# Hybrid attention encoder layer: a planner that tells an engine's occupation from the lag of its result

## The chip, the cores and the metric

The kernel runs on one core of a Trainium2 chip. The metric is the device time of one execution in microseconds (us). Before the change three runs took 2861.65, 2861.87 and 2867.31 us; their median is 2861.87 us. One more execution was profiled, and every row shown below is of that one.

## The reference, cut to what matters

The layer takes two sequences, `x_sample` of 2048 tokens and `x_prompt` of 512, each with 1024 features, and one set of weights. Everything is float32.

```python
h = rms_norm(x, norm_gain)
proj = h @ w_in                          # 1024 -> 9216, split in 16 parts
q_a, k_a = rms_norm per head             # 8 heads of 64
o_a = neighborhood_attention(q_a, k_a, v_a, rel_bias_a)   # 8 rows x 16 columns of a grid of width 64
for (window, dil) in ((128, 1), (512, 4), (2048, 16)):    # three dilated groups
    q, k = rope(rms_norm(...))
    o, lse = sliding window attention over tokens of stride dil
o_b = sum over groups of softmax(lse) * o
br_a = (o_a * silu(g_a)) @ w_branch_a    # 512 -> 1024
br_b = (o_b * silu(g_b)) @ w_branch_b
merged = sigmoid(m_a) * br_a + sigmoid(m_b) * br_b
y = x + merged @ w_out                   # 1024 -> 1024
```

## The kernel before, in words

**Stages.** `run` (L2065) calls four sweeps. `dil_sweeps` takes tiles of 128 tokens, 20 for each of the three dilated groups; for each it makes three products of 512 columns (q, k, v) and the attention of the tokens that are complete by then. `na_sweeps` takes 40 tiles (two halves of four heads, 20 tiles each) with a q-and-k product of 512 columns and a v product of 256, and the neighbourhood attention. `gate_sweeps` makes gates and branch products in blocks of 256 tokens, `out_sweep` the last product. The float32 products are made as three products of 16-bit parts (a high and a low part of each side), so that one bank of 512 columns over 1024 features is 24 matmuls.

**What a q or k tile passes through** (`dil_qk`, L1390): TensorE fills a PSUM tile `proj` (four exist). ScalarE copies it to `qk` and squares it to `sq` (these two give the `proj` tile back), VectorE sums the squares (`q_ssq`), GpSimd turns it by the rope tables (two halves `sq<-qk,gcs`, then `qk<-qk,gcs`, then `qk<-qk,sq`), computes the last step of the inverse root on small tiles (`q_c`, `q_t`, `q_y`) and scales (`qk<-qk,q_y`); ScalarE writes the high half `qs`, VectorE or GpSimd the low half, and a transposing DMA on SyncE's queue carries `qs` to `dq` or `kT`. Three `qk` tiles exist.

**What a unit of attention passes through** (`head` L764, `softmax` L801, `pump` L854): the scores go to a PSUM tile `s` (two exist); VectorE adds the mask and takes the maximum (a custom instruction, `e<-s,cmask` or `e<-s,bm`), ScalarE or VectorE makes `neg`, ScalarE takes exp in place, ScalarE or VectorE writes the high half `p`, VectorE or GpSimd the low half (two `e` tiles exist; one is held from the maximum to here), a transposing DMA carries `p` to `pT` (six exist), and the products with v go to `o`.

**What sets the order of the work.** The order of instructions on each engine is the order in which the Python program emits them; nothing reorders it afterwards, and each engine takes its own instructions strictly in that order. The program finds the order with a model of time, `Clock`. The sweeps emit TensorE's matmuls one after the other and advance `clk.t` by each one's cost (`pe`, L130). Every other step is an event on a heap: it is emitted when TensorE's model time has passed the time at which the step's inputs are ready (`at` L119, `then` L123, `catch_up` L148). `run` (L134) books a step on its engine: the engine is taken for the step's cost, and the result is ready a lag after that; the next step of the chain becomes an event at that time (`done`). Buffers (`Slots`) are given back in model time too, and `first` (L144) chooses between two engines by which would be done first. `dma` (L138) books an issue on the queue, then a cost on one shared resource `D`, then a lag. So the constants of the model change no instruction's work; they change where a step stands among others on its engine, and now and then which of two engines takes a step.

**Names that the steps below use.** `mm` L351 (cost of a matmul), `act` L359, `vec` L364, `pool` L376, `copy` L368 and `either` L380 (the two that choose an engine), `turn` L398 (transposing DMA), the margins `M_T = 0.5` (before a transpose of `p`) and `M_PV = 1.5` (after it, before the product with v), and the pace of units of attention, `DIL_STEP` and `NA_STEP`. None of the margins and paces is touched. All helper lines of the profile (L352, L360, L365, L377, L400) lie in these functions, so that groups are told apart by their tiles.

Of the kernel before, what the change touches and what calls it, by code (L numbers as in the profile page):

```python
# [13 lines left out]
F32 = mybir.dt.float32  # L14
# [11 lines left out]
D = 1024  # L26
# [59 lines left out]
NA_P = 0.7  # L86
DIL_STEP = 1.3
DIL_1 = 0.8
LAG_A = 0.6
LAG_V = 0.35  # L90
LAG_P = 0.2
LAG_D = 1.2
A_DMA = 0.1
NA_ACT = 0
# [9 lines left out]
PORT = 0.18  # L104
BIAS_STEP = 4.0
LAG = {"A": LAG_A, "V": LAG_V, "P": LAG_P, "D": LAG_D}


class Clock:
# [25 lines left out]
        self.free[e] = max(self.now, self.free[e]) + cost  # L135
        self.done = self.free[e] + LAG[e]

    def dma(self, e, issue, cost):  # L138

        self.free[e] = max(self.now, self.free[e]) + issue  # L140
        self.free["D"] = max(self.free[e] + 0.7, self.free["D"]) + cost
        self.done = self.free["D"] + LAG["D"]

    def first(self, **costs):  # L144

# [29 lines left out]
class Slots:  # L175
# [37 lines left out]
    def new(self, pool, shape, dtype, names):  # L213

        i = self.granted.popleft()
        pool = self.pools.get(i, pool)
        if i in self.views:
            ts = [self.views[i]]
        else:
            ts = [pool.tile(shape, dtype, name=self.names.get(i, f"{n}{i}"), bufs=1) for n in names]  # L220
        self.where[self.key(ts[0])] = i
        return ts
# [38 lines left out]
def size(ap):  # L261
    return math.prod(ap.shape[1:])


class Enc:
# [84 lines left out]

    def mm(self, out, a, b, start, stop, share=1, **kw):  # L351
        self.nc.tensor.matmul(out, a, b, start=start, stop=stop, **kw)  # L352
        self.clk.pe((size(b) * (4 if b.dtype == F32 else 1) / 2400 + 0.003) / share)

    def tp(self, out, x, m=128):
        self.nc.tensor.transpose(out, x, self.ident[:m, :m])
# [2 lines left out]
    def act(self, out, x, func=AF.Copy, **kw):  # L359
        self.nc.scalar.activation(out, x, func, **kw)  # L360
        by_row = not isinstance(kw.get("scale", 1.0), float) or "bias" in kw
        self.clk.run("A", 0.155 + size(out) / 1200 + 0.135 * by_row + 0.28 * ("accum_out" in kw))

    def vec(self, ins, /, out, *a, n=None, more=0.0, **kw):  # L364
        getattr(self.nc.vector, ins)(out, *a, **kw)  # L365
        self.clk.run("V", 0.15 + (n or size(out)) / 960 + 0.08 * ("accum_out" in kw) + more)

    def copy(self, out, x):  # L368

        n = size(out)  # L370
        if self.clk.first(A=0.155 + n / 1200, V=0.15 + n / 1920 + PORT) == "A":
            self.act(out, x)
        else:
            self.vec("tensor_copy", out, x, n=n / 2, more=PORT)

    def pool(self, ins, /, out, *a, n=None, **kw):  # L376
        getattr(self.nc.gpsimd, ins)(out, *a, **kw)  # L377
        self.clk.run("P", 0.23 + (n or size(out)) / 480)

    def either(self, ins, /, out, *a, n=None, **kw):  # L380

        n = n or size(out)
        if self.clk.first(V=0.15 + n / 960 + PORT, P=0.23 + n / 480) == "V":
            self.vec(ins, out, *a, n=n, more=PORT, **kw)
        else:
            self.pool(ins, out, *a, n=n, **kw)
# [11 lines left out]
    def turn(self, out, in_):  # L398

        self.nc.sync.dma_start(out=out, in_=in_, transpose=True)  # L400
        n = math.prod(out.shape)
        self.clk.dma("S", max(1.23, n / 107e3), n / 82e3)

    def new(self, name, shape, dtype=F32, pool=None, names=None):
        ts = self.S[name].new(pool or self.P.get(name) or self.ps, shape, dtype, names or (name,))
# [317 lines left out]
    def split_v(self, R, ps, nh, pool, name, then):  # L723

        clk = self.clk
        ps3 = ps.rearrange("p (h d) -> p h d", d=64)

        def high():
            R["v"], = self.S[name].new(pool(), [128, nh, 2, 64], FP16, (name,))
            self.act(R["v"][:, :, 0], ps3, scale=VP)  # L730
            clk.then(low)

        def low():
            self.vec("scalar_tensor_tensor", R["v"][:, :, 1], ps3, VP, R["v"][:, :, 0], op0=ALU.mult,
                     op1=ALU.subtract)
            self.S["proj"].give(ps)
            clk.then(then)

        self.S[name].take(high)
# [61 lines left out]
    def softmax(self, u):  # L801
# [33 lines left out]
        def low():  # L835
            p = u["p"]
            self.either("tensor_tensor", p[:m, N:2 * N], u["e"][:m, :N], p[:m, :N], op=ALU.subtract)
            S["e"].give(u["e"])
            clk.at(clk.done + M_T, S["pT"].take, turn)
# [166 lines left out]
    def na_qk(self, R, seq, i, ps):  # L1006
# [102 lines left out]
        moved.when(lambda: S["qs"].give(R["qs"]))  # L1109
        there.when(groups)  # L1110
        S["qk"].take(copy)

    def na_group(self, seq, g):
# [276 lines left out]
    def dil_qk(self, R, i, ps):  # L1390
# [51 lines left out]
        def low():  # L1442
            self.either("tensor_tensor", *B["parts"][1], op=ALU.subtract)
            S["qk"].give(B["x"])
            clk.then(R["place", i].when, turn)

        def turn():
# [3 lines left out]
            R["ch"]["done"][R["i"]].signal()  # L1451

        S["qk"].take(copy)

    def dil_v(self, R, ps):
# [212 lines left out]
    def gate_o(self, H, br, blk):  # L1668
# [27 lines left out]
        def low(tt, o, qs):  # L1696
            self.either("tensor_tensor", qs[:, 512:1024], o, qs[:, 0:512], op=ALU.subtract)
            S["x"].give(o)
            clk.then(turn, tt, qs)
# [476 lines left out]
```

## Time and profile before

| what | value |
|---|---|
| median of three runs | 2861.87 us |
| the profiled execution's own time | 2864.63 us |
| its span, first to last instruction | 2862.8 us |
| TensorE busy | 2675.4 us (93%) |
| GpSimd, VectorE, ScalarE busy | 1474.7, 1576.5, 1334.6 us |
| chain of waits, share by engine | PE 65%, DVE 9%, POOL 8%, DMA 7%, ACT 6% |
| mean granted TensorE clock | 0.971 |

In the rows PE is TensorE's matmuls, PEld its weight loads, DVE VectorE, ACT ScalarE, POOL GpSimd and SPq SyncE's queue, which issues all the DMAs. Times are from the start of the span. The sweeps of the dilated groups fill the span up to some 1245 us, the neighbourhood attention up to some 1806 us, the gates up to 2636 us, the last product the rest. A row of the view of waits says who sat idle until whose result came, for how long in total, how often, and the longest.

### The profile page before, as it was taken

How to read it: one execution, taken by the hardware profiler on the slowest of the kernel's cores; microseconds unless marked ns; L12 is line 12 of the kernel's file. 1: busy time of each engine (PE TensorE's matmuls, PEld its weight loads, DVE VectorE, ACT ScalarE, POOL GpSimd, SP SyncE). 2: the span in 40 equal slices, each digit the busy share in tenths (PEclk: the TensorE clock that was granted, in tenths of full speed). 3: DMA queues.
4: the chain of work that ended last, by engine and by line, in shares of the span. 5: the costliest groups of instructions: out<-in, count | busy, mean ns of one | idle time of the engine just before them, and what ended most of it. 6: DMA issues, size and time to landing. Idle time of an engine off the chain costs nothing.

```text
span 2862.8 us, 55914 instructions
## 1 busy us (share of the span) xinstructions
PE 2675.4 (93%) x20841; PEld 1788.6 (62%) x20841; DVE 1576.5 (55%) x3670; ACT 1334.6 (47%) x3561; POOL 1474.7 (52%) x1991
## 2 busy tenths in 40 slices
PE   5998989989999999999898886899999999999999
PEld 2444444444444444455455554889999999999887
DVE  7777666775655764557676687332145444454111
ACT  5666666665666665656666667221123121122010
POOL 4987768677778888756676664000012121131110
PEclk9999999999999999999999996899999999999999
DMA  7999886766675755588998897332144344353443
GB/s 208 223 214 195 176 196 110 158 127 119 114 121 114 156 114 115 98 224 182 192 226 190 180 206 169 85 71 75 45 129 159 109 128 133 110 172 118 148 139 110
DMA packets 808017, 419.21 MB, mean 146 GB/s; under 512 B 689728, under 2 KB 734400, under 8 KB 801344
## 3 DMA queue, kind: packets, MB, share of 16 engines
q1 hardware_dynamic: 807744, 415.63, 62.9%
q8 instruction: 163, 2.67, 0.4%
q14 instruction: 110, 0.90, 0.1%
HBM read 171.72 MB, written 79.13 MB: 88 GB/s over the span
## 4 chain that ended last, share of the span: by engine, by line
PE 65%; DVE 9%; POOL 8%; DMA 7%; ACT 6%; issue 4%; SPq 1%; DVEq 0%; POOLq 0%; ACTq 0%
PE proj L352 54%; PE s L352 10%; POOL qk L377 4%; DMA pT<-p 4%; PE o L352 2%; DVE p L365 2%; ACT e L360 2%; DVE e L365 2%; POOL sq L377 2%; DMA qn<-qs 1%; POOL q_t L377 1%; ACT sq L360 1%; DVE wm L365 1%; DVE q_ssq L365 1%; ACT qk L360 1%
## 5 line engine op out<-in xcount | busy, mean ns | idle before, releaser
L352 PEld LDWEIGHTS <-hb 128*128 128x128 f16 x6240 | 591.6, 99 | 684.6 <-issue 124.8
L352 PE MATMUL proj<-wt,hb 128*128 128x512 f16 (+2 forms) x3360 | 688.0, 357 | 26.1 <-ACT sq L360 18.0
L352 PE MATMUL proj<-wu,hb 128*128 128x512 f16 x2880 | 668.4, 385 | 45.1 <-ACT sq L360 30.5
L360 ACT ACTIVATE sg<-proj,wi 128x256 f32<-128x256 f32 x240 | 113.1, 473 | 639.3 <-PE proj L352 629.7
L360 ACT ACTIVATE e<-e,neg,sc 128x256 f32<-128x256 f32 (+4 forms) x688 | 393.4, 574 | 8.4 <-DVE neg L365 4.5
L352 PE MATMUL proj<-hb,wt 128*128 128x256 f16 x2760 | 313.7, 274 | 5.0 <-DMA hb<-htd 2.1
L352 PEld LDWEIGHTS <-pT 128*128 128x128 f16 (+1 forms) x4560 | 227.7, 102 | 139.1 <-DMA pT<-p 64.1
L352 PEld LDWEIGHTS <-wt 128*128 128x128 f16 x2760 | 269.3, 98 | 39.4 <-issue 4.0
L377 POOL TENSOR_TENSOR qk<-qk,sq 128x512 f32<-128x512 f32 (+1 forms) x141 | 183.9, 1304 | 196.2 <-DVE qk L365 100.7
L365 DVE TENSOR_TENSOR p<-e,p 128x512 f16<-128x512 f32 (+2 forms) x278 | 248.1, 893 | 63.4 <-ACT p L360 59.6
L377 POOL TENSOR_TENSOR sq<-qk,gcs 128x256 f32<-128x256 f32 x240 | 191.4, 818 | 135.6 <-DVE q_ssq L365 128.9
L365 DVE TENSOR_TENSOR qk<-s,sg 128x256 f32<-128x256 f32 x160 | 67.7, 424 | 348.1 <-PE s L352 345.6
L352 PE MATMUL s<-hb,wt 128*128 128x256 f32 x1880 | 246.9, 285 | 0.0
L352 PE MATMUL proj<-hb,kT 128*128 128x256 f16 x1920 | 228.2, 276 | 5.2 <-ACT sg L360 2.7
L352 PEld LDWEIGHTS s<-hb,wt 128*128 128x128 f32 x1880 | 231.2, 189 | 0.9
L377 POOL TENSOR_TENSOR hb<-sg,hb 128x256 fp32r<-128x256 f32 x65 | 54.0, 831 | 341.3 <-ACT hb L360 341.3
L365 DVE CUSTOM_DVE_ANT_0 e<-s,cmask 128x256 f32<-128x256 f32 (+2 forms) x528 | 154.3, 344 | 107.1 <-PE s L352 90.2
L352 PEld LDWEIGHTS <-kT 128*128 128x128 f16 x1920 | 184.4, 99 | 30.5 <-DVE kT L365 3.5
L365 DVE CAST p<-e 128x512 f16<-128x512 f32 (+2 forms) x182 | 120.1, 660 | 131.4 <-ACT e L360 109.5
L377 POOL TENSOR_TENSOR qk<-qk,q_y 128x512 f32<-128x512 f32 x160 | 179.2, 1124 | 5.2
L377 POOL TENSOR_TENSOR qk<-qk,gcs 128x512 f32<-128x512 f32 x120 | 167.0, 1391 | 9.4
L352 PE MATMUL proj<-wv,hb 128*128 128x512 f16 x660 | 156.6, 383 | 8.3 <-ACT sq L360 6.9
(181 smaller groups left out, 3774.9 us busy)
## 6 DMA issues: line engine op xcount, KB each, us to landing
hb<-htd SPq DMA_DIRECT2D x40, 1024.0 KB
wr<-in_w_in SPq DMA_DIRECT2D x132, 256.0 KB
obd<-osb SPq DMA_DIRECT2D x50, 264.0 KB
hd<-xs SPq DMA_DIRECT2D x20, 512.0 KB
htd<-hb SPq DMA_DIRECT2D x10, 1024.0 KB
mad<-qk SPq DMA_DIRECT2D x40, 256.0 KB
e<-obd SPq DMA_DIRECT2D x40, 256.0 KB
sq<-mad SPq DMA_DIRECT2D x40, 256.0 KB
```

Of the source, the lines that this page charges most:

```text
L352: self.nc.tensor.matmul(out, a, b, start=start, stop=stop, **kw)
L360: self.nc.scalar.activation(out, x, func, **kw)
L365: getattr(self.nc.vector, ins)(out, *a, **kw)
L377: getattr(self.nc.gpsimd, ins)(out, *a, **kw)
```

## The change

The lags of the three engines' results fall (ScalarE 0.6 to 0.13 us, VectorE 0.35 to 0.115, GpSimd 0.2 to 0.125), and so do the fixed parts of their costs (0.155 to 0.06, 0.15 to 0.07, 0.23 to 0.19). A transposing DMA takes the shared resource for less time (elements / 82e3 to / 105e3) and has a lag of its own of 0.2 us in place of 1.2; other DMAs keep theirs. Every matmul costs the model 4% more.

```diff
-LAG_A = 0.6
-LAG_V = 0.35
-LAG_P = 0.2
+
+LAG_A = 0.13
+LAG_V = 0.115
+LAG_P = 0.125
 LAG_D = 1.2
...
-    def dma(self, e, issue, cost):
+    def dma(self, e, issue, cost, lag=LAG_D):
 
         self.free[e] = max(self.now, self.free[e]) + issue
         self.free["D"] = max(self.free[e] + 0.7, self.free["D"]) + cost
-        self.done = self.free["D"] + LAG["D"]
+        self.done = self.free["D"] + lag
...
-        self.clk.pe((size(b) * (4 if b.dtype == F32 else 1) / 2400 + 0.003) / share)
+        self.clk.pe((size(b) * (4 if b.dtype == F32 else 1) / 2400 + 0.003) * 1.04 / share)
...
-        self.clk.run("A", 0.155 + size(out) / 1200 + 0.135 * by_row + 0.28 * ("accum_out" in kw))
+        self.clk.run("A", 0.06 + size(out) / 1200 + 0.135 * by_row + 0.28 * ("accum_out" in kw))
...
-        self.clk.run("V", 0.15 + (n or size(out)) / 960 + 0.08 * ("accum_out" in kw) + more)
+        self.clk.run("V", 0.07 + (n or size(out)) / 960 + 0.08 * ("accum_out" in kw) + more)
...
-        if self.clk.first(A=0.155 + n / 1200, V=0.15 + n / 1920 + PORT) == "A":
+        if self.clk.first(A=0.06 + n / 1200, V=0.07 + n / 1920 + PORT) == "A":
...
-        self.clk.run("P", 0.23 + (n or size(out)) / 480)
+        self.clk.run("P", 0.19 + (n or size(out)) / 480)
...
-        if self.clk.first(V=0.15 + n / 960 + PORT, P=0.23 + n / 480) == "V":
+        if self.clk.first(V=0.07 + n / 960 + PORT, P=0.19 + n / 480) == "V":
...
-        self.clk.dma("S", max(1.23, n / 107e3), n / 82e3)
+        self.clk.dma("S", max(1.23, n / 107e3), n / 105e3, 0.2)
```

## Rows read from the trace of the kernel before

**Rows 1.** The page's first part: busy time, share, instructions of each engine.

```profile
PE 2675.4 (93%) x20841; PEld 1788.6 (62%) x20841; DVE 1576.5 (55%) x3670; ACT 1334.6 (47%) x3561; POOL 1474.7 (52%) x1991
```

**Rows 2.** Busy time by stretch: start:end, length, engines, granted clock, DMA share, GB/s.

```profile
0.00:100.00 100.00, 69.34 (x334) 30.56 (x335) 69.56 (x157) 57.88 (x130) 58.40 (x75) 0.95 0.76 211
100.00:600.00 500.00, 450.23 (x3305) 220.96 (x3305) 358.40 (x823) 328.68 (x875) 393.48 (x526) 0.97 0.84 178
600.00:1245.00 645.00, 624.04 (x4673) 309.67 (x4667) 380.47 (x1045) 393.09 (x1189) 515.57 (x735) 0.99 0.63 120
1245.00:1650.00 405.00, 368.58 (x3066) 210.67 (x3066) 274.69 (x665) 250.19 (x677) 265.39 (x409) 0.97 0.92 201
1650.00:1806.00 156.00, 111.15 (x1110) 72.88 (x1109) 115.66 (x278) 107.65 (x275) 81.71 (x91) 0.73 0.89 184
1806.00:2862.80 1056.80, 1052.05 (x8366) 943.85 (x8363) 377.70 (x705) 197.12 (x418) 160.16 (x160) 1.00 0.38 115
```

**Rows 3.** TensorE's waits in 100:600, 600:1245, 1245:1650 and 1650:1806, in this order.

```profile
PE proj L352 <- ACT sq L360: 37.6, 16, 5.8
...
PE proj L352 <- ACT sq L360: 11.0, 8, 3.4
...
PE o L352 <- DMA pT<-p: 19.8, 22, 3.6
...
PE o L352 <- DMA pT<-p: 22.0, 20, 2.7
PE s L352 <- DVE mx L365: 12.5, 11, 2.1
```

**Rows 4.** ScalarE's waits in 100:1245.

```profile
ACT neg L360 <- DVE osb L365: 183.1, 139, 6.7
ACT qs L360 <- POOL qk L377: 80.1, 44, 5.9
ACT qk L360 <- PE proj L352: 72.9, 31, 5.6
```

**Rows 5.** Timeline about 172 us: start, length, instruction, [idle before it and who ended that].

```profile
165.69 4.70 PE L352 MATMUL proj<-wu,hb 128*128 128x512 f16 x21
...
171.08 2.06 DVE L365 SCALAR_TENSOR_TENSOR xs<-x,x_y,xs 128x1024 f16<-128x1024 f32 x1
...
172.04 1.23 POOL L377 TENSOR_SCALAR q_c<-q_ssq,wi 128x8 f32<-128x8 f32 x1
172.09 0.63 ACT L360 ACTIVATE qs<-qk 128x512 f16<-128x512 f32 x1 [4.02 <-POOL qk L377]
172.62 0.58 ACT L360 ACTIVATE qk<-proj 128x512 f32<-128x512 f32 x1
...
173.74 2.53 PE L352 MATMUL proj<-wu,hb 128*128 128x512 f16 x11 [3.00 <-ACT sq L360]
```

**Rows 6.** Groups by line and shape: count | busy us, mean ns | idle before.

```profile
L360 ACT ACTIVATE qk<-proj 128x512 f32<-128x512 f32 x160 | 93.2, 583 | 89.5 <-PE proj L352 84.3 <-POOL qs L377 5.0
...
L377 POOL TENSOR_TENSOR qk<-qk,gcs 128x512 f32<-128x512 f32 x120 | 167.0, 1391 | 9.4
...
L377 POOL TENSOR_SCALAR q_c<-q_ssq,wi 128x8 f32<-128x8 f32 x160 | 68.6, 429 | 30.4 <-DVE q_ssq L365 30.3
...
L365 DVE TENSOR_TENSOR p<-e,p 128x512 f16<-128x512 f32 x207 | 190.7, 921 | 40.0 <-ACT p L360 36.9
```

**Rows 7.** Timeline about 443 us: a transposing DMA and the matmuls that waited for it.

```profile
441.13 1.20 SPq L400 DMA_TRANSPOSE pT<-p  x1
...
443.83 0.56 PE L352 MATMUL o<-dv,pT 128*64 128x64 f16 x12 [2.36 <-DMA pT<-p]
```

**Rows 8.** Busy time of the instructions that touch the tiles `proj`, 1740 to 1760 us.

```profile
1740.00:1760.00 20.00, 0.00 (x0) 0.00 (x0) 0.00 (x0) 0.00 (x0) 0.50 0.75 146
```

**Rows 9.** Timeline about 1723 us: first and last step of a unit on its `e` tile.

```profile
1721.81 0.69 DVE L365 CUSTOM_DVE_ANT_0 e<-s,bm 128x512 f32<-128x512 f32 x1
...
1724.88 0.69 DVE L365 TENSOR_TENSOR p<-e,p 128x512 f16<-128x512 f32 x1
```

## The prediction, made before the changed kernel was built or timed

> **What bounds the kernel now.** I read the busy times first, then the stretches, then who waited for whom in each, then single waits in the timeline. TensorE is busy for 2675.4 of 2862.8 us [rows 1], so all that a better order of the same work can win is its idle time, 187.4 us, and some of the time at the lower granted clock. The stretches say where that lies [rows 2]. From 1806 us on, 1052.1 of 1056.8 us are busy at a granted clock of 1.00: no order helps there. The first 100 us lose 30.7 us, in the chain that loads and scales the first weights. What is left are three parts. The dilated groups lose 49.8 us in 100:600 and 21.0 us in 600:1245. The neighbourhood attention loses 36.4 us in 1245:1650, where the DMA engines are busy for 0.92 of the time. Its tail, 1650:1806, loses 44.9 us of 156.0, and the mean clock granted there is 0.73: much of it runs at 1.2 GHz in place of 2.4.
>
> The waits name the causes [rows 3]. In the dilated groups TensorE waits for ScalarE's square of an earlier q or k tile, which gives a `proj` tile back: 16 + 8 waits, 48.6 us, 2.0 us each. In the neighbourhood attention it waits for transposed `pT` (22 + 20 waits, 41.8 us, 1.0 us each), and in the tail also for the maximum that gives an `s` tile back (12.5 us). Why is the square late? ScalarE takes its instructions in order and stands idle for 183.1 us before `neg`, until VectorE's maximum, and for 80.1 us before `qs`, until GpSimd's scaling [rows 4]. One case shows it [rows 5]: the matmuls of a bank end at 170.39, yet the copy and square that empty it stand behind a `qs` whose data GpSimd has ready only at 172.09, after 4.02 us of idling; TensorE loses 3.00 us. So the order on ScalarE matters, and it comes from the model.
>
> **The change, part by part.** No instruction's work changes; each part moves steps in the order.
>
> *How near the new constants are.* For 512 columns ScalarE's result now comes 0.487 + 0.13 = 0.62 us after its start, before 0.582 + 0.6 = 1.18; the row has 583 ns [rows 6]. GpSimd's product: 1.257 + 0.125 = 1.38, before 1.50; row 1391 ns. VectorE's low half: 0.783 + 0.115 = 0.90, before 1.21; row 921 ns. Only GpSimd's smallest steps are off: 0.33 against 429 ns. A half-size transpose: 1.23 + 0.7 + 0.62 + 0.2 = 2.75 us from issue to landing, before 3.93; the trace has 443.83 - 441.13 = 2.70 [rows 7]. Step by step the new model is the better one. It knows no contention, though, and no late neighbour.
>
> *Chains.* Summing a unit of two heads of 256 keys from score to product with v (0.2 from TensorE, two maxima, `neg`, two exps, high, low, `M_T`, transpose, `M_PV`) gives 13.7 us by the old constants and 9.9 by the new. The product with v therefore moves forward by up to 3.8 us among TensorE's matmuls. A q or k tile from bank to `qs` low: 12.4 us old, 10.0 new; `qs` and the rest move forward by 2.4 us on ScalarE, past evictions of later banks.
>
> *The dilated groups.* Where a step becomes ready earlier in the model, its buffer is given back earlier and the next tile is planned more tightly; ScalarE's evictions then stand behind fewer planned bursts. Bound of the gain: 183.1 of the 263.2 us that ScalarE idles [rows 4] is for VectorE, whose results the new constants place right (0.90 against 0.921); if that share of the 48.6 us goes, 34 us. Bound of the loss: `qs` moves forward by 2.4 us while GpSimd's data come no earlier; if half as many evictions again are caught as now (12 more at 2.0 us), 24 us. Between the two I take **-6 us**, close to the middle, since nothing in the rows lies nearer to one end.
>
> *Products with v.* They come up to 3.8 us sooner, and TensorE may get to them ahead of the transpose. In 600:1245 none waits for `pT`; in the attention 42 wait, 1.0 us each. A shift that is the same for all is paid once (3.8 us), since TensorE, once late, is late for everything after. Bounds: 0, and 27 more waits of 1.0 us. I take **+4 us**, the single payment.
>
> *The attention's tail.* A unit of 512 keys holds one of two `e` tiles from maximum to low half: by the old constants 1.11 + 0.89 + 1.60 + 1.18 + 1.21 = 6.0 us, by the new 0.80 + 0.33 + 1.03 + 0.62 + 0.90 = 3.7. The trace has 1721.81 to 1725.57, 3.8 us [rows 9]. So the old model could start a pair of units every 6.0 us at most, although `NA_STEP` asks for one every 4.6, and the units it could not place among the projections were left for the end: from 1740 to 1760 no instruction touches a `proj` tile [rows 8], TensorE has attention alone. With 3.7 us the pace of 4.6 decides, and a quarter of the backlog moves back to where TensorE has projections to do. A quarter of the tail's idle 44.9 us is 11 us, and the half clock gives back some more: **-14 us**. Bounds: the whole 44.9 us; and +10, if the DMA engines, 0.92 and 0.89 busy, can't take the units earlier and they wait there instead.
>
> *Parts without a price.* The choice between engines: `either` prefers VectorE by 0.474 us in place of 0.434, `copy` prefers ScalarE by 0.03 in place of 0.015; a few steps of some 0.9 us go to VectorE, which is busy for 274.7 of 405 us in the fullest attention stretch: hidden, and if that cover is gone, 1 us each. The 4% on matmuls makes the model's TensorE slower against the other engines and undoes a little of the shift (0.2 us in a bank of 24). The lower cost on `D` lets transposes follow each other sooner in the model; SyncE's queue and its issue costs are as before. In 1245:1650 I expect nothing either way, with 20 us on both sides, as the DMA share is 0.92. The clock: each stall avoided spares some of the time at the lower level, **-2 us** (granted 0.97 in 100:600 [rows 2]).
>
> **Sum:** -6 + 4 - 14 - 2 = -18 us on the profiled execution's 2864.6, so 2846.6. That execution lies 2.8 us above the median of 2861.87, so the forecast against the median is 2844 us, -0.6%. A measurement of this kernel can tell about 0.2%, 6 us, from no change.
>
> **The rivals.**
>
> *No change that can be told.* A constant shift is paid once and the stretches from 1806 on and 600:1245 are full (624.0 of 645.0 us busy). For it: the waits are spread over few places. Against it: the tail's idle time and the `e` tiles' 6.0 us. Time: 2862 plus or minus 6. Chance 0.19.
>
> *Slower: evictions caught behind `qs`.* The place is ScalarE's queue in the dilated groups. `qs` stands 2.4 us earlier, GpSimd delivers no earlier, and each further eviction caught costs the 2.0 us of today's; it decides the run if more than 12 further evictions of the 120 are caught than `neg` sets free. For it: 44 waits of `qs` already [rows 4], and GpSimd's steps stretch beside VectorE: its 128x8 step took 1.23 us at 172.04 while VectorE's two-input `xs` ran from 171.08 to 173.14 [rows 5], against a mean of 429 ns [rows 6]; the new constants make GpSimd faster yet. Against it: ScalarE idles more for VectorE than for GpSimd. Price: 24 us from the bound above and 4 from the products with v, so 2890. Chance 0.22. The Trainium skill, "GPSIMD Engine Reference", section 1 (Specifications), says that GpSimd shares its SBUF interfaces with VectorE and contends with VectorE's instructions of two SBUF inputs; by that rule a fixed, lower cost for GpSimd is wrong wherever VectorE works beside it, which speaks against this change. The trace agrees, by the 1.23 us.
>
> *Slower: TensorE ahead of its transposes.* 27 further waits of 1.0 us, with nothing won: 2889. For it: in the attention 42 products with v wait already. Against it: none does in 600:1245. Chance 0.11.
>
> *Much faster.* The tail's idle time and VectorE's share of the dilated stalls go whole, 45 + 34 us less the 4: some 2787; half of it 2824. Chance 0.08.
>
> *The change does not do what it says*: only the selection of engines moves. That is the case of no change, and counted there.
>
> **How the numbers follow.** My forecast, a gain between 6 and 40 us, has 0.40; with the much faster case 0.48 are on the faster side, 0.19 are the same, 0.22 + 0.11 = 0.33 slower. The likeliest case's own range is 2822 to 2856. For 8 in 10 I go from 2800, halfway into the much faster case, to 2893, which takes in both slower rivals at their price; some 0.08 lie below and some 0.1 above.
>
> **What would show it.** Right: idle TensorE in 1650:1806 (or its counterpart) below 35 us, fewer microseconds between the last `proj` matmul of the attention and the first of the gates, a pair of units every 4 to 5 us, the end stretch as before at some 1055 us. TensorE's waits for ScalarE's square in the dilated groups at 35 to 45 us. Wrong: these waits over 60 us with ScalarE's wait for GpSimd before `qs` over 100 us (the first slower rival), or waits for `pT` in 600:1245 (the second), or the tail as long as before with the DMA share still near 0.9.

## The result: slower by 2.6%, and the profile after

The changed kernel takes 2940.68 us (median of four runs, 2940.18 to 2941.52) against 2863.98 us for the kernel before in four runs beside it: a ratio of 1.026 (95% interval 1.0247 to 1.0273), 77 us more. The forecast was 2844 us in a range of 2800 to 2893, so both the sign and the range are wrong.

Busy times and the chain that ended last, from the page of the kernel after, against [rows 1]:

```profile
PE 2694.2 (92%) x20841; PEld 1791.3 (61%) x20841; DVE 1602.0 (54%) x3794; ACT 1341.4 (46%) x3551; POOL 1349.4 (46%) x1876
...
PE 45%; DVE 17%; POOL 12%; ACT 11%; DMA 8%; issue 7%; SPq 2%; DVEq 0%; ACTq 0%; POOLq 0%
```

TensorE runs the same 20841 matmuls. Its idle time grew from 187.4 to 2939.7 - 2694.2 = 245.5 us, by 58.1 us; it was also busy for 18.8 us longer, and no experiment shows why. TensorE's share of the chain fell from 65% to 45%: VectorE, GpSimd and ScalarE together went from 23% to 40%. No engine became the bound; TensorE stands more often behind chains of the others.

Where in the span? First the busy times by stretch (columns as in [rows 2]), cut where the same work ends now:

```profile
100.00:600.00 500.00, 436.88 (x3233) 212.54 (x3233) 351.60 (x810) 318.46 (x865) 354.17 (x478) 0.95 0.80 168
600.00:1294.00 694.00, 645.90 (x4694) 315.50 (x4694) 376.44 (x1061) 404.18 (x1203) 528.88 (x767) 0.98 0.60 117
1294.00:1700.00 406.00, 351.91 (x2908) 200.18 (x2903) 289.04 (x679) 241.78 (x646) 234.54 (x359) 0.96 0.86 194
1700.00:1880.00 180.00, 137.65 (x1329) 89.08 (x1329) 132.53 (x305) 114.91 (x297) 104.63 (x129) 0.89 0.84 180
1880.00:2939.70 1059.70, 1052.22 (x8364) 943.59 (x8361) 387.94 (x794) 204.76 (x417) 72.65 (x70) 1.00 0.38 114
```

Then the first and last start of some of TensorE's groups: the last projection of q and k for the dilated groups (`proj<-wu,hb`), their last scores (`s<-kT,dq`), the scores of the neighbourhood attention (`s<-kT,qT`) and the branch products of the gates (`s<-hb,wt`). The columns are the shortest, median and longest duration in ns, then the first and last start in us. In the kernel before:

```profile
L352 PE MATMUL proj<-wu,hb x2880: 376/379/635, 22.8 to 1217.2; 128*128 128x512 f16 x192
L352 PE MATMUL s<-hb,wt x1880: 274/281/562, 1806.5 to 2636.2; 128*128 128x256 f32 x188
...
L352 PE MATMUL s<-kT,dq x1584: 212/227/418, 83.2 to 1245.7; 64*128 64x256 f16 x90, 64*128 64x128 f16 x72, 64*64 64x128 f16 x36
L352 PE MATMUL s<-kT,qT x384: 319/376/631, 1295.8 to 1759.4; 64*128 64x384 f16 x96, 64*128 64x512 f16 x96
```

and after:

```profile
L353 PE MATMUL proj<-wu,hb x2880: 376/379/634, 17.7 to 1279.3; 128*128 128x512 f16 x192
L353 PE MATMUL s<-hb,wt x1880: 274/281/561, 1880.1 to 2713.0; 128*128 128x256 f32 x188
...
L353 PE MATMUL s<-kT,dq x1584: 212/236/418, 84.4 to 1294.4; 64*128 64x256 f16 x90, 64*128 64x128 f16 x72, 64*64 64x128 f16 x36
L353 PE MATMUL s<-kT,qT x384: 319/373/631, 1352.8 to 1813.7; 64*128 64x384 f16 x96, 64*128 64x512 f16 x96
```

The 77 us fall into four parts. Up to the first neighbourhood score 1352.8 - 1295.8 = 57.0 us are lost, 48.7 of them by the last dilated score (1245.7 to 1294.4). From the first to the last neighbourhood score the two take the same, 463.6 and 460.9 us. From there to the first branch product it is 47.1 before and 66.4 after, 19.3 more. The rest loses 3.3. So most of the loss lies in the dilated groups, where the forecast had a small gain.

Who makes TensorE wait there? Its waits over the whole span, before (columns: whose result, us in total, times, longest):

```profile
PE proj L352 <- ACT sq L360: 55.5, 27, 5.8
PE o L352 <- DMA pT<-p: 45.3, 44, 3.6
PE s L352 <- DVE mx L365: 18.6, 19, 2.1
PE proj L356 <- DVE wm L365: 16.8, 2, 15.7
...
PE s L352 <- DVE osb L365: 1.5, 1, 1.5
PE s L352 <- DMA kT<-qs: 0.3, 1, 0.3
```

and after:

```profile
PE o L353 <- DMA pT<-p: 61.2, 56, 3.2
PE s L353 <- DVE mx L366: 47.8, 49, 3.4
PE proj L357 <- DVE wm L366: 43.2, 14, 14.1
PE s L353 <- DVE osb L366: 25.9, 26, 4.1
PE s L353 <- DMA kT<-qs: 19.9, 18, 4.1
...
PE proj L353 <- ACT sq L361: 1.7, 2, 1.4
```

The stall from which the forecast started, a `proj` tile waiting for ScalarE's square [rows 3], is gone: 55.5 to 1.7 us. What took its place is larger. Waits for VectorE's maxima, which give an `s` tile back (`mx` in the neighbourhood attention, `osb` in the dilated groups), rose from 20.1 to 73.7 us; waits for a transposed `kT` from 0.3 to 19.9; for `pT` from 45.3 to 61.2. Waits of small matmuls for VectorE's maxima of the weights (`wm`) rose from 16.8 to 43.2, in several stages; no experiment singles them out.

ScalarE's waits in the dilated groups (100:1294), against [rows 4]:

```profile
ACT neg L361 <- DVE osb L366: 184.8, 149, 4.8
ACT qs L361 <- POOL qk L378: 121.0, 52, 6.6
```

and VectorE's there, first before (100:1245), then after (100:1294):

```profile
DVE p L365 <- ACT e L360: 96.9, 76, 3.4
...
DVE q_ssq L365 <- ACT sq L360: 82.1, 51, 8.0
DVE qs L365 <- ACT qs L360: 60.0, 44, 5.0
```

```profile
DVE p L366 <- ACT e L361: 133.3, 100, 2.3
DVE qs L366 <- ACT qs L361: 100.6, 50, 8.9
DVE q_ssq L366 <- ACT sq L361: 95.9, 59, 4.8
```

All of VectorE's waits for ScalarE in this stage sum to 289 us before and 385 after. VectorE stands longer in front of results that ScalarE has not given yet, and its later steps stand behind it. One case in the timeline of the kernel after shows how that reaches TensorE:

```profile
203.86 0.20 POOL L378 TENSOR_TENSOR q_y<-q_y,q_t 128x8 f32<-128x8 f32 x1
...
204.13 0.83 PE L353 MATMUL s<-kT,dq 64*128 64x256 f16 x12
204.20 0.68 DVE L366 SCALAR_TENSOR_TENSOR dv<-proj,dv 128x512 f16<-128x512 f32 x1
...
204.37 1.41 POOL L378 TENSOR_TENSOR sq<-qk,gcs 128x256 f32<-128x256 f32 x2 [0.30 <-DVE q_ssq L366]
...
204.90 4.06 PE L353 MATMUL proj<-wu,hb 128*128 128x512 f16 x18
...
209.73 2.04 POOL L378 TENSOR_TENSOR qk<-qk,q_y 128x512 f32<-128x512 f32 x2
...
210.81 0.63 ACT L361 ACTIVATE qs<-qk 128x512 f16<-128x512 f32 x1 [5.37 <-POOL qk L378]
...
211.47 0.85 DVE L366 TENSOR_TENSOR qs<-qk,qs 128x512 f16<-128x512 f32 x1 [6.59 <-ACT qs L361]
212.25 0.41 DVE L366 CUSTOM_DVE_ANT_0 e<-s,cmask 128x256 f32<-128x256 f32 x1
...
213.06 0.37 PE L353 MATMUL s<-kT,dq 64*128 64x256 f16 x1 [4.11 <-DVE osb L366]
```

Scores are ready at 204.96, and VectorE is free from 204.88. But next in its order is the low half of `qs`, which needs ScalarE's high half, which needs GpSimd's scaling: VectorE idles 6.59 us, ScalarE 5.37 us, and the maximum that would free the `s` tile starts at 212.25, 7.3 us after its data. TensorE finishes its 18 matmuls and stands for 4.11 us. No step in these rows is unusually long; what costs is the place of `qs` in the order of VectorE and of ScalarE. GpSimd's order takes part: the factor `q_y` of this tile is there at 204.06, but the next tile's rotation, which runs from 204.37 on, stands ahead of the scaling. That alone isn't what the change brought: by the order in which the programs emit, 50 of the 120 scalings of the dilated groups stand behind a later tile's rotation before, and 40 after.

### The profile page after: what moved, and what is told of

Its sections match the earlier page's. It is cut to its first block, busy times and chain, and to the rows that moved or that the text cites. A ratio compares the mean times of both kernels' runs of the same rounds, so it can differ in the third digit from the quotient of the medians.

```text
span 2939.7 us, 55826 instructions
## 1 busy us (share of the span) xinstructions
PE 2694.2 (92%) x20841; PEld 1791.3 (61%) x20841; DVE 1602.0 (54%) x3794; ACT 1341.4 (46%) x3551; POOL 1349.4 (46%) x1876
## 4 chain that ended last, share of the span: by engine, by line
PE 45%; DVE 17%; POOL 12%; ACT 11%; DMA 8%; issue 7%; SPq 2%; DVEq 0%; ACTq 0%; POOLq 0%
PE proj L353 35%; PE s L353 8%; POOL qk L378 6%; ACT e L361 5%; DVE e L366 4%; DVE p L366 4%; DMA pT<-p 3%; POOL sq L378 2%; DVE wm L366 2%; DVE wt L366 2%; POOL q_t L378 1%; DVE q_ssq L366 1%; DVE qs L366 1%; DMA kT<-qs 1%; ACT qs L361 1%
## 5 line engine op out<-in xcount | busy, mean ns | idle before, releaser
L378 POOL TENSOR_TENSOR sq<-qk,gcs 128x256 f32<-128x256 f32 x240 | 185.1, 792 | 191.2 <-DVE q_ssq L366 184.4
L366 DVE TENSOR_TENSOR p<-e,p 128x512 f16<-128x512 f32 (+2 forms) x277 | 237.0, 861 | 58.0 <-ACT p L361 54.1
L378 POOL TENSOR_TENSOR qk<-qk,sq 128x512 f32<-128x512 f32 (+1 forms) x131 | 167.9, 1281 | 159.8 <-DVE qk L366 146.4
L366 DVE CAST p<-e 128x512 f16<-128x512 f32 (+2 forms) x225 | 136.4, 607 | 176.7 <-ACT e L361 171.9
L366 DVE TENSOR_TENSOR qs<-qk,qs 128x512 f16<-128x512 f32 (+1 forms) x151 | 129.1, 858 | 128.0 <-ACT qs L361 123.2
L361 ACT ACTIVATE qs<-qk 128x512 f16<-128x512 f32 (+1 forms) x200 | 106.8, 537 | 165.0 <-POOL qk L378 164.9
L366 DVE TENSOR_REDUCE q_ssq<-sq 128x8 f32<-128x512 f32 x160 | 108.9, 681 | 116.8 <-ACT sq L361 116.2
```

## The experiments

All ratios are to the kernel before, with 95% intervals; "us back" counts against the 2940.7 of the kernel after. In the diffs A, V, P stand for ScalarE, VectorE, GpSimd.

**Lags or fixed costs?** Each half was put back alone.

```diff
-LAG_A = 0.13
-LAG_V = 0.115
-LAG_P = 0.125
+LAG_A = 0.6
+LAG_V = 0.35
+LAG_P = 0.2
```

> The changed kernel with the three lags of ScalarE, VectorE and GpSimd as before (0.6, 0.35, 0.2); the lower costs, the transposes and the 4% stay changed. Theory 1, the short lags took away the cushion behind which TensorE's small matmuls stood: most of the 77 us comes back, 2865 to 2885 us, and TensorE's waits for VectorE's maximum (s tiles, 74 us after the change) fall below 35 us. Theory 2, the lower costs overbook VectorE and move steps from GpSimd to it: it stays near 2930. Theory 3, the transposes are planned too early: it stays near 2920, waits for pT stay near 61 us.

Measured: 2875.3 us, 1.0035 (1.0023 to 1.0046). The waits for the maxima fall from 73.7 to 31.2 us, as theory 1 asks; those for `pT` rise to 92.0.

```diff
-        self.clk.run("A", 0.06 + size(out) / 1200 + 0.135 * by_row + 0.28 * ("accum_out" in kw))
+        self.clk.run("A", 0.155 + size(out) / 1200 + 0.135 * by_row + 0.28 * ("accum_out" in kw))
-        self.clk.run("V", 0.07 + (n or size(out)) / 960 + 0.08 * ("accum_out" in kw) + more)
+        self.clk.run("V", 0.15 + (n or size(out)) / 960 + 0.08 * ("accum_out" in kw) + more)
-        self.clk.run("P", 0.19 + (n or size(out)) / 480)
+        self.clk.run("P", 0.23 + (n or size(out)) / 480)
```

The constants in `copy` and `either` go back in the same way.

> The changed kernel with the fixed costs of ScalarE, VectorE and GpSimd as before (0.155, 0.15, 0.23, in the choices between engines too); lags, transposes and the 4% stay changed. Theory 1 (lags): little comes back, 2915 to 2940. Theory 2 (costs): back to 2865 to 2885, GpSimd's instructions back from 1876 to about 1990. Theory 3 (transposes): near 2930.

Measured: 2864.06 us, 1.0000 (0.9991 to 1.0009). Either half alone brings back nearly everything: 65 and 77 us. GpSimd's instructions rise to 1958, so that the signs of theories 1 (in e1) and 2 (here) both came true. Neither lags nor costs did the harm by themselves; the loss needs both to be short.

**Transposes and matmuls.**

```diff
-        self.clk.dma("S", max(1.23, n / 107e3), n / 105e3, 0.2)
+        self.clk.dma("S", max(1.23, n / 107e3), n / 82e3, 1.2)
```

> The changed kernel with the transposing DMA's cost and lag as before (elements / 82e3, 1.2 us). Theory 1 (lags) and theory 2 (costs): 10 to 20 us come back, 2920 to 2930, as TensorE's waits for pT (61 us) and kT (20 us) shrink to half. Theory 3 (transposes): 2865 to 2885.

Measured: 2923.7 us, 1.0203 (1.0182 to 1.0224). TensorE's waits for `pT` fall from 61.2 to 37.5 us, and those for `kT` from 19.9 to 3.4; those for `mx` rise from 47.8 to 72.0, and those for the square from 1.7 to 30.8. Most of what is saved in one wait is lost in another, and 17 us come back.

```diff
-        self.clk.pe((size(b) * (4 if b.dtype == F32 else 1) / 2400 + 0.003) * 1.04 / share)
+        self.clk.pe((size(b) * (4 if b.dtype == F32 else 1) / 2400 + 0.003) / share)
```

> The changed kernel without the 4% on a matmul's cost. If the 4% holds the model's TensorE back behind the other engines, so that their results look ready for it, taking it out lets TensorE run ahead in the model and its matmuls stand later among the others' steps: 2915 to 2930. Theories 1 to 3 by themselves say nothing of it: 2935 to 2945, within 0.2% of the changed kernel.

Measured: 2934.99 us, 1.024 (1.0222 to 1.0259), 6 us back, between the two ranges.

**Slack ahead of TensorE only.** If TensorE merely comes too early to its tiles, margins at those points should give the time back.

```diff
-M_PV = 1.5
+M_PV = 3.5
-M_W1 = 0.6
+M_W1 = 2.6
...
-        self.S = {n: Slots(clk, b) for n, b in (("proj", 4), ("s", 2), ("o", 2))}
+        self.S = {n: Slots(clk, b, m) for n, b, m in (("proj", 4, 0.0), ("s", 2, 1.5), ("o", 2, 0.0))}
...
-        t = max(clk.done, self.unit_at)
+        t = max(clk.done + 1.5, self.unit_at)
```

> The changed model, with margins ahead of TensorE's small matmuls alone: an s tile is given back 1.5 us later in the model, the product with v waits 3.5 us after its transpose in place of 1.5, the weights' maxima 2.6 in place of 0.6, a dilated unit's scores 1.5 us more after its keys. Theory A, the loss arises in TensorE's own queue, where matmuls stand ahead of late results: 2865 to 2885 us, TensorE's waits for pT, the maxima, kT and the weights' maxima (208 us after the change) under 100. Theory B, the steps on ScalarE, VectorE and GpSimd are in a worse order among themselves: 2915 to 2940, and other waits of TensorE (for proj tiles) take their place.

Measured: 2940.75 us, 1.0261 (1.0246 to 1.0276): nothing back. TensorE's waits in this kernel:

```profile
PE s L353 <- DVE mx L366: 48.1, 57, 4.1
PE o L353 <- DMA pT<-p: 37.5, 42, 4.4
...
PE s L353 <- DVE osb L366: 32.8, 35, 3.0
...
PE s L353 <- DMA kT<-qs: 22.3, 13, 3.4
```

The waits for `pT` fell, and so did those for `wm` (from 43.2 to 23.6), the two places that had a margin of 2 us. The maxima are as late as ever, and VectorE's waits for ScalarE in the dilated groups rose from 385 to 426 us: the lateness arises ahead of TensorE. A cure at the place of the symptom did nothing.

**Which engine's numbers?** Cost and lag of one engine put back, in `copy` and `either` too, the rest new.

```diff
-LAG_V = 0.115
+LAG_V = 0.35
...
-        self.clk.run("V", 0.07 + (n or size(out)) / 960 + 0.08 * ("accum_out" in kw) + more)
+        self.clk.run("V", 0.15 + (n or size(out)) / 960 + 0.08 * ("accum_out" in kw) + more)
```

> The changed kernel with VectorE's cost and lag alone as before (0.15 and 0.35, in the choices too). If the loss comes from VectorE's steps, planned too early and too many (its maxima hold the s tiles): 2870 to 2890, GpSimd's instructions back towards 1990. If any lost cushion weighs alike, a third to a half comes back: 2900 to 2915.

Measured: 2925.91 us, 1.0218 (1.0201 to 1.0235), 15 us back. GpSimd has 1986 of its former 1991 instructions here: the steps that moved from it to VectorE aren't what cost the 77 us.

```diff
-LAG_A = 0.13
+LAG_A = 0.6
...
-        self.clk.run("A", 0.06 + size(out) / 1200 + 0.135 * by_row + 0.28 * ("accum_out" in kw))
+        self.clk.run("A", 0.155 + size(out) / 1200 + 0.135 * by_row + 0.28 * ("accum_out" in kw))
```

> The changed kernel with ScalarE's cost and lag alone as before (0.155 and 0.6). If the loss comes from VectorE's steps: 2920 to 2940. If it comes from the whole chain's length, of which ScalarE's lags are the most (0.565 us for each of its steps, five in a unit): 2870 to 2890.

Measured: 2861.2 us, 0.9985 (0.9974 to 0.9995): all of it, more than either theory allowed. TensorE's waits:

```profile
PE o L353 <- DMA pT<-p: 67.7, 69, 3.6
...
PE s L353 <- DVE mx L366: 24.5, 32, 1.7
PE proj L353 <- ACT sq L361: 18.3, 9, 4.7
...
PE s L353 <- DVE osb L366: 7.6, 11, 2.0
...
PE s L353 <- DMA kT<-qs: 3.6, 5, 1.2
```

The maxima fall from 73.7 to 32.1 us and `kT` from 19.9 to 3.6; VectorE's waits for ScalarE in the dilated groups fall from 385 to 303 us, and the first neighbourhood score stands at 1289.5 us (before 1295.8, after 1352.8).

```diff
-LAG_P = 0.125
+LAG_P = 0.2
...
-        self.clk.run("P", 0.19 + (n or size(out)) / 480)
+        self.clk.run("P", 0.23 + (n or size(out)) / 480)
```

> The changed kernel with GpSimd's cost and lag alone as before (0.23 and 0.2, together 0.115 us for a step). Little by any theory, 2925 to 2945; if the loss is in GpSimd's late scaling ahead of qs (ScalarE's wait 97 us before, 165 after), 2890 to 2910.

Measured: 2924.89 us, 1.0207 (1.0192 to 1.0222), 16 us back.

**ScalarE's numbers from both sides.** Its lag alone, its cost alone (with `copy`'s), and the reverse: the kernel before with only ScalarE's numbers new.

```diff
-LAG_A = 0.13
+LAG_A = 0.6
```

> The changed kernel with ScalarE's lag alone as before (0.6), its cost new (0.06). Theory C, VectorE's steps stand in its queue ahead of ScalarE results that the model promises too early: the lag alone brings back nearly what cost and lag together did, 2860 to 2885 us, and VectorE's waits for ScalarE in the dilated groups fall from 385 us to under 340. Theory D, ScalarE's load matters (how many steps the model thinks it can take): 2910 to 2935.

Measured: 2876.29 us, 1.0037 (1.0023 to 1.0052), 64 us back; VectorE's waits for ScalarE fall to 331 us. Both are as theory C asks.

```diff
-        self.clk.run("A", 0.06 + size(out) / 1200 + 0.135 * by_row + 0.28 * ("accum_out" in kw))
+        self.clk.run("A", 0.155 + size(out) / 1200 + 0.135 * by_row + 0.28 * ("accum_out" in kw))
-        if self.clk.first(A=0.06 + n / 1200, V=0.07 + n / 1920 + PORT) == "A":
+        if self.clk.first(A=0.155 + n / 1200, V=0.07 + n / 1920 + PORT) == "A":
```

> The changed kernel with ScalarE's cost alone as before (0.155, in the choices too), its lag new (0.13). Theory C (results promised too early; here 0.095 us later for a step): a small part comes back, 2910 to 2930. Theory D (ScalarE's load): 2860 to 2885.

Measured: 2884.03 us, 1.007 (1.0053 to 1.0087), 57 us back. That is theory D's range, so e9 and e10 don't decide between the two theories: both numbers of ScalarE count. This edit also moves some copies from ScalarE to VectorE, so it is not the cost alone.

The last of these, against the kernel before:

```diff
-LAG_A = 0.6
+LAG_A = 0.13
...
-        self.clk.run("A", 0.155 + size(out) / 1200 + 0.135 * by_row + 0.28 * ("accum_out" in kw))
+        self.clk.run("A", 0.06 + size(out) / 1200 + 0.135 * by_row + 0.28 * ("accum_out" in kw))
-        if self.clk.first(A=0.155 + n / 1200, V=0.15 + n / 1920 + PORT) == "A":
+        if self.clk.first(A=0.06 + n / 1200, V=0.15 + n / 1920 + PORT) == "A":
```

> The kernel before with ScalarE's new cost and lag alone (0.06 and 0.13), all else as before. If ScalarE's two numbers alone make the loss: 2910 to 2945. If the loss needs the others too (the chain has to be short everywhere): 2865 to 2890.

Measured: 2929.04 us, 1.0223 (1.0208 to 1.0239). ScalarE's two numbers alone make some 64 of the 77 us. The waits for the maxima are 49.2 + 12.6 = 61.8 us, VectorE's waits for ScalarE 409 us. The waits for the square, though, stay at 54.2 us: ScalarE's numbers alone bring the loss and not the gain that the forecast was after.

**Is it the hand-over from ScalarE to VectorE?** Half a microsecond of margin, only where VectorE (or GpSimd) takes up ScalarE's result: square to sum, exp to high half, high half to low half.

```diff
+M_AV = 0.5
...
-            clk.then(S["p"].take, high)
+            clk.at(clk.done + M_AV, S["p"].take, high)
...
-            clk.then(low)
+            clk.at(clk.done + M_AV, low)
...
-            clk.then(reduce)
+            clk.at(clk.done + M_AV, reduce)
...
```

> The changed model with 0.5 us more at three hand-overs from ScalarE alone: square to sum of squares, exp to high half, high half to low half (p, and q and k tiles). Theory C: 2870 to 2900, VectorE's waits for ScalarE in the dilated groups under 340 us. Theory D: 2915 to 2940.

Measured: 2889.49 us, 1.0088 (1.0073 to 1.0103): 51 us back, two thirds, with all constants new. VectorE's waits for ScalarE fall from 385 to 358 us only. So slack at these points cures most of the loss, but the sum of these waits isn't a full measure of it, and theory C's sign of under 340 us failed. Since the margins lengthen the planned chain as well, this run doesn't tell the hand-over from the chain's length.

```diff
-LAG_V = 0.115
+LAG_V = 1.0
```

> The changed kernel with VectorE's lag at 1.0 in place of 0.115, more cushion on one engine than any kernel here had on ScalarE. If only the length of the chain counts: back to 2865 to 2890. If it is ScalarE's results promised too early, ahead of which VectorE's steps stand: 2905 to 2940, and VectorE's waits for ScalarE in the dilated groups stay over 350 us.

Measured: 2902.07 us, 1.0135 (1.0121 to 1.0149): 39 us back, just below the second range; VectorE's waits for ScalarE stay at 380 us, as it asks. Slack on VectorE helps too, but nearly four times the excess over the new lag that it had before ((1.0 - 0.115) / (0.35 - 0.115)) gives 39 of 77 us only.

**How much slack?** The lag of ScalarE alone, between and beyond the two values; from 0.9 on with ScalarE's old cost as well, in `copy` too.

```diff
-LAG_A = 0.13
+LAG_A = 0.35
```

> The changed kernel with ScalarE's lag at 0.35, near half way from 0.13 to 0.6. If the loss grows evenly with the missing lag: 2900 to 2915. If there is a threshold: near 2876 or near 2940.

Measured: 2896.51 us, 1.012 (1.0104 to 1.0136): 44 us back, somewhat more than an even growth would give. With e9 the dose is graded, without a threshold: 0.13 gives 2940.7, 0.35 gives 2896.5, 0.6 gives 2876.3.

```diff
-LAG_A = 0.13
+LAG_A = 0.9
...
-        self.clk.run("A", 0.06 + size(out) / 1200 + 0.135 * by_row + 0.28 * ("accum_out" in kw))
+        self.clk.run("A", 0.155 + size(out) / 1200 + 0.135 * by_row + 0.28 * ("accum_out" in kw))
```

> ScalarE's cost as before (0.155) and its lag at 0.9, beyond the old 0.6, the rest as changed (2861 us with 0.6). If more cushion helps further: 2840 to 2855. If 0.6 was at the best point: 2862 to 2885, as TensorE waits for proj tiles again.

Measured: 2848.69 us, 0.995 (0.9937 to 0.9964). This version beats both kernels, by 0.5% and 3.1%. The first neighbourhood score stands at 1272.3 us.

The same with one step more:

```diff
-LAG_A = 0.9
+LAG_A = 1.2
```

> As at 0.9 (2849 us), with ScalarE's lag at 1.2. If the cushion still pays: 2835 to 2846. If 0.9 is past the best point or at it: 2850 to 2875, with TensorE's waits for ScalarE's square (18 us at 0.6) over 40 us.

Measured: 2871.97 us, 1.0021 (1.0011 to 1.0031). Past 0.9 more slack costs again, but not by the expected wait: TensorE's waits for the square are 24.1 us, not over 40.

The same lag in the kernel before, with all else as it was there:

```diff
-LAG_A = 0.6
+LAG_A = 0.9
```

> The kernel before with ScalarE's lag at 0.9 in place of 0.6. If the longer lag alone is the gain: 2845 to 2856. If the gain needs the other engines' measured constants, since before every result was late enough: 2860 to 2880.

Measured: 2877.23 us, 1.0033 (1.0021 to 1.0044). With the other constants old, 0.9 is worse than 0.6. So the good point of e16 belongs to that set of constants and not to ScalarE's lag alone.

**By stage.** The constants of e7 in the dilated groups, all of the kernel before's from the neighbourhood attention on.

```diff
+C = {"V": 0.07, "P": 0.19, "M": 1.04, "T": 105e3, "TL": 0.2}
+OLD = {"V": 0.15, "P": 0.23, "M": 1.0, "T": 82e3, "TL": 1.2}
...
+            C.update(OLD)
+            LAG.update(V=0.35, P=0.2)
...
-        self.clk.dma("S", max(1.23, n / 107e3), n / 105e3, 0.2)
+        self.clk.dma("S", max(1.23, n / 107e3), n / C["T"], C["TL"])
```

> ScalarE's cost and lag as before everywhere; VectorE, GpSimd, transposes and the 4% as changed in the dilated groups (1231 us long there, against 1245 before) and as before from the neighbourhood attention on (569 against 561). If the stages add up: 2850 us, 0.4% faster than before. If the later stage only inherits what the earlier left: 2858 to 2870.

Measured: 2866.27 us, 1.0013 (1.0004 to 1.0021), against 0.9985 for e7: the stages don't add up, and the attention's own old constants win nothing.

## Why the prediction was wrong, step by step

**The step that failed** is the term of the dilated groups, "Between the two I take -6 us", where 57.0 us were lost by the first neighbourhood score; and under it the sentence "Step by step the new model is the better one". The constants of most steps are indeed nearer to their instructions (not those of GpSimd's smallest steps, 0.45 us before and 0.33 now for 429 ns). But a lag in this planner does more than stand for a delay: it decides where the next step of a chain stands in an engine's strict order. The planner's own times, printed as it emits, show what was lost. For a dilated unit of 256 keys, in the median of 120 such units from the end of the scores to the end of the low half, it had 7.6 us by the old constants, and the trace of the kernel before has 7.2; by the new constants it has 5.4, and the trace of the kernel after has 9.2. The new constants are near the single steps and too short for the chain, which also waits in queues behind work that the model doesn't have there. The plan for the dilated groups ends at 1230 us by the old constants (in the trace their last scores start at 1245.7), at 1176 by the new (1294.4).

That the old plan and its execution agree so well isn't what makes a kernel quick. Taken in the same way, e7, e2 and e16 have 7.3, 7.2 and 8.1 us planned but 8.9, 9.8 and 9.0 executed, as long as in the kernel after. What goes with the time is the planned length: the ten kernels of this case with 6.4 us or more take 2849 to 2889 us, the ten with less than 6.2 take 2884 to 2941. That is a comparison over the kernels, no test by itself.

That ScalarE's two numbers decide most of it is shown: e7 gives all back, e12 alone makes most of the loss, e14 and e9 grade it, e11 gives two thirds back with margins at the hand-overs to VectorE and GpSimd. They aren't the only cure, as e2 returns all three engines' fixed costs and gives everything back with the short lags. That the time passes through VectorE's queue, as in the case at 204 us, is shown for that case and fits the totals (289 to 385 us of waits, `s` waits from 20.1 to 73.7), but it isn't shown to be the whole path. VectorE's idle time ahead of ScalarE's results while finished scores of a dilated unit stood in their `s` tile was 11.2 us before and 51.0 after; yet it is 51.9 in e1 and 41.1 in e2, which lost little or nothing. GpSimd's waits for VectorE before its rotation (`sq<-q_ssq`) rose as well, from 124.0 to 180.6 us, and how the loss divides between these two queues stays open.

**The bounds of that step** were too narrow for a reason. The gain was bounded by 34 of 48.6 us, by way of ScalarE's idle time for VectorE; that idle time stayed (183.1 to 184.8 us), and the waits for the square vanished all the same. ScalarE's numbers didn't do it (e12); with the old transposes 30.8 us of them are left (e3), with VectorE's old numbers 24.6 (e6). The loss was bounded by 24 us, from evictions behind `qs` on ScalarE alone. The same event on VectorE, a maximum caught behind the low half of `qs` or `p`, was not priced, though [rows 4] shows ScalarE idling for 183.1 us until VectorE's maximum: a sign that VectorE's order matters too. Up to the first neighbourhood score the loss came to 57.0 us, in place of a gain of 6.

**Products with v, +4 (0 to +27).** The waits for `pT` rose by 16 us, 13.4 of them in 600:1294 where there were none: inside the bounds, and more than a single payment. They weren't what counted: e5 cuts them to 37.5 us and gains nothing, and e7 has 67.7 us of them and loses nothing.

**The attention's tail, -14 (-44.9 to +10).** The first half of the mechanism happened and paid nothing. The projections of the attention now reach to its end: the last starts at 1798.6 us, before at 1670.3 (the group `proj<-wt,hb`, taken from 1300 to 1770 us before and from 1350 to 1870 after, so that its first start is where the cut lies):

```profile
L352 PE MATMUL proj<-wt,hb x1488: 272/330/635, 1299.7 to 1670.3; 128*128 128x512 f16 x93, 128*128 128x256 f16 x93
```

```profile
L353 PE MATMUL proj<-wt,hb x1569: 272/379/634, 1349.8 to 1798.6; 128*128 128x256 f16 x99, 128*128 128x512 f16 x98
```

What lies behind it up to the first branch product shrank from 136 to 82 us, and the stretch at the low clock with it (granted 0.73 in [rows 2], 0.89 in the last stretch before the gates now). But the last projection now comes 445.8 us after the first neighbourhood score in place of 374.5, and TensorE waits 46 times for the maximum (45.9 us) by then. From the first to the last score the planner has 453 us by the old constants and 415 by the new; executed it was 463.6 before, 460.9 after, and 444 to 476 in the experiments. So "With 3.7 us the pace of 4.6 decides" failed: the model's pace changed, the executed one hardly did. What holds the executed pace isn't shown. The 19.3 us after the last score came on top: 192 matmuls of the gates' first projections (26.3 us) run there now, which before started at 1679.3 us, ahead of the last score.

**Clock, -2.** The mean granted clock is 0.973, before 0.971: no gain that can be told. The attention's end has more of it, 100:600 less (0.97 to 0.95).

**Parts without a price.** The choice moved more steps than "a few": GpSimd has 115 instructions fewer and VectorE 124 more. It cost next to nothing, as said: from the first branch product on 1056.3 us became 1059.6, and in e6 and e12 GpSimd has 1986 and 1971 instructions, nearly as before, and most of the loss is there all the same.

**The rivals.** Of the first slower one the sign on `qs` came true (ScalarE's wait for GpSimd rose from 80.1 to 121.0 us), but its price didn't: the wait of `proj` for the square was to rise above 60 us and is 1.7. It named the late step and the wrong queue. GpSimd's own constants, to which the contention with VectorE spoke, gave 16 of the 77 us back (e8). The second, TensorE ahead of its transposes, happened in part, and e5 took its price away without a gain.

**What stays open.** Returned one at a time, the constants give 80 (ScalarE), 15, 16, 17 and 6 us, over 130 in all of a loss of 77: they don't add. Among sets of constants that all plan a long chain (e2, e7, e15 to e18) the time still varies between 2849 and 2877 us, and no run shows a rule for it. By which queues the short plan costs its time, beyond single cases, is open too.

## What to carry to other kernels

A lag in a planner that fixes an in-order schedule is a cushion as well as a latency: constants that were nearer to most single steps made a slower kernel here. Look at the planned length of a whole chain (7.6 us from scores to low half before, 5.4 after) and compare planned and executed ends of each stage (1176 us against a last score at 1294.4) before trusting a "more exact" model. How much cushion is best has to be found by runs: the quickest kernel here plans 8.1 us, and e17 and e18 with 8.7 and 8.6 are slower. When a stall on one engine's queue is priced, price the same event on every queue that the moved step passes. Change the constants of one engine at a time: 3% lay between the best and the worst of the sets tried here.

## What was not expected of the hardware

VectorE took over 89 steps in the gates and the last product (705 to 794 instructions) for 10 us of busy time (377.7 to 387.9 us), while GpSimd lost 90 steps and 87.5 us. VectorE's other steps became shorter meanwhile. The product `sq<-qk,qk` from 1806 us on, before, and from 1880 us on, after (count | busy us, mean ns):

```profile
L365 DVE TENSOR_TENSOR sq<-qk,qk 128x256 f32<-128x256 f16 x37 | 28.8, 779 | 0.0
```

```profile
L366 DVE TENSOR_TENSOR sq<-qk,qk 128x256 f32<-128x256 f16 x39 | 17.7, 454 | 0.0
```

These means mix two durations. In the kernel before, 12 of the 37 run with GpSimd idle and take 409 to 424 ns; the other 25 run beside an instruction of GpSimd and take 951 to 959 ns, with nothing between. One of the 25:

```profile
2216.18 0.72 POOL L377 TENSOR_TENSOR hb<-sg,hb 128x256 fp32r<-128x256 f32 x1 [1.29 <-ACT hb L360]
2216.23 0.95 DVE L365 TENSOR_TENSOR sq<-qk,qk 128x256 f32<-128x256 f16 x1
```

In the kernel after, 36 of the 39 run with GpSimd idle, at 407 to 417 ns. The Trainium skill, "GPSIMD Engine Reference", section 1 (Specifications), says that GpSimd contends with VectorE's instructions of two SBUF inputs; the trace agrees, with 0.95 us beside GpSimd against 0.42 alone. So in a stage where both have room, a step moved from GpSimd to VectorE may cost less than its own length; here TensorE was the bound, and the last stages took no less time.
